# Decay levels of a gated linear attention, two at a time, with their subtractions on GpSimd

## The chip, the cores and the metric

One core of one Trainium2 chip runs the kernel. The metric is device microseconds from start to end of one execution; the time before is the median of three runs.

## The reference, cut to what matters

A two-layer encoder trunk on 256 tokens of width 1024. Each layer is a half-step SwiGLU block, a mixer, and another half-step SwiGLU block, all with RMS normalization and a residual. The mixer of layer 0 is a bidirectional gated linear attention with 4 heads (key width 128, value width 256); that of layer 1 is a differential softmax attention. The change touches only the mixer of layer 0:

```
b = cumsum(log_a)                       # per head and key column, log_a <= 0
o_i = sum over j<=i of (q_i * exp(b_i - b_j)) . k_j v_j     # forward
# backward: the same on flipped tokens, with its own gate and j<i
# then: o = rms_norm(o_f + o_b) * silu(g) @ w_out
```

## The kernel before, in words

All weights stream from HBM as float32 tiles (`stage`, three buffers) and are split into a high and a low half, so that TensorE can multiply in a faster format with three products: ScalarE writes the high half and VectorE the low half (both at line 192, `issue`, made by `parts`), into `w` tiles with five buffers. `next_weights` loads and splits ahead, up to LOOK_SPLIT = 3 weights beyond the one in use (`split_weights`, line 177). `state["hold"]` can keep back low halves until a `release`.

In `gla` the two heads of a pair (`hp` 0 or 1) and the two blocks of 128 tokens are laid side by side. The decays exp(b_i - b_j) are not formed for all pairs i, j. Tokens whose positions in a block first differ at bit s are handled as level s: both q and k are multiplied by the exponential of their distance to the middle of their group of 2s tokens, and one product of q and k gives the scores of that level. There are levels 64, 32, 16, 8, 4, 2, 1 inside a block and a level 128 across the blocks, in the order of GLA_LEVELS, "64 32 16 128 8 4 2 1", for hp 0 and then for hp 1: 16 levels. Each has three steps:

- `d` (`decay`, line 685): the differences of prefix sums go to the tile `arg` (line 710; line 706 for level 1, two smaller ones), then ScalarE writes exponentials to `qkd` (lines 712 and 713, or 707), a tile with three buffers. Level 128 needs no differences.
- `l` (`level_scores`, line 716): VectorE multiplies `qkd` by q and k (line 721; 719 for level 1), and TensorE makes eight 128-column products in one PSUM tile (`scores`, line 681).
- `t` (`take`, line 726): VectorE (line 735) or ScalarE copies the part of the scores that belongs to the level into `sd` or `sx`.

The order in which all this is issued is written out by hand in GLA_ORDER. `h` is the next half group of the projections: for v and g a half group is 12 multiplications of 512 columns (lines 231 to 233), four to a group: v0, g0, v1, g1 (v0/0 is the first of v0). `p0` and `p1` make the prefix sums (copied by ScalarE at line 669), `r0` and `r1` the raw scores, `a0` and `a1` the product with v and its sums of squares (`attend`; statistics at line 756, then a chain of small VectorE steps), `hold` sets low halves to wait, and behind the bar `x` releases them, `g0`/`g1` are gates, `o0` normalizes (line 804, then transposes at line 811). TensorE, VectorE, ScalarE and GpSimd each work through their own queue in order.

Of the kernel before, what the change touches and what calls it, by code (L numbers as in the profile page):

```python
# [11 lines left out]
F32 = mybir.dt.float32  # L12
# [3 lines left out]
ALU = mybir.AluOpType  # L16
AX = mybir.AxisListType

P = 128
# [6 lines left out]
GH, DK, DV = 4, 128, 256  # L26
# [25 lines left out]
GLA_COLS = "q0 k0 q1 k1 v0 g0 v1 g1"  # L52
GLA_LEVELS = "64 32 16 128 8 4 2 1"
GLA_ORDER = """
h z h y h h h h p0 h p1 h r0 d h d l h d l h t d l h t d l h t d r1 h t d l l h d l h t t d l h t l d h t d d h t l l a0 t d l h t d l h t hold d l h t d l t l t t | g0 h x a1 o0 h g1
"""

DIFF_COLS = "a0 a1 a2 b0 a3 v2 v3"
# [62 lines left out]
def trunk(ctx: ExitStack, tc: tile.TileContext, ins, out):  # L121
    nc = tc.nc
# [77 lines left out]
    def next_weights():  # L200
        n = state["use"]
        state["use"] += 1
        prefetch(n)
        split_weights(n)
        return split.pop(n)
# [110 lines left out]
    x = xpool.tile([P, KD, T], F32, tag="x", name="x")  # L316
# [277 lines left out]
    def gla(norm, nxt, w2):  # L594
        QK = KD // 2
        with ExitStack() as gctx:
# [5 lines left out]
            z = gp.tile([P, 4, 512], F32, tag="v", name="z")  # L602
            la = gp.tile([P, 4, 512], F32, tag="g", name="la")
            with tc.tile_pool(name="glb", bufs=2) as lp:

                lr = lp.tile([P, T], FR, tag="lr", name="lr", bufs=1)
                bias = lp.tile([P, 2, GH * DK], F32, tag="arg", name="bias", bufs=1)
                nc.sync.dma_start(bias, ins["gla_b_gate"][0].rearrange("a b -> (a b)").partition_broadcast(P))
                state["hold"] = "low"
                w = next_weights()  # L610
# [74 lines left out]
                def decay(hp, level):  # L685

                    a = lp.tile([P, 2, 4, P], F32, tag="qkd", name=f"qkd{level}_{hp}", bufs=3)
                    if level == P:
                        pf, pb = pre[:, hp, 0], pre[:, hp, 1, :, 1 : P + 2]
                        for b in range(2):  # L690
                            g0, g1 = 2 * b, 2 * b + 1
                            nc.scalar.activation(a[:, 0, g0, :], pb[:, g0, 0:P], AF.Exp, scale=-1.0, bias=pb[:, g0, P : P + 1])
                            nc.scalar.activation(a[:, 1, g0, :], pf[:, g0, 1 : P + 1], AF.Exp, scale=-1.0, bias=pf[:, g0, P : P + 1])
                            nc.scalar.activation(a[:, 0, g1, :], pf[:, g1, 1 : P + 1], AF.Exp)
                            nc.scalar.activation(a[:, 1, g1, :], pb[:, g1, 0:P], AF.Exp)
                        return a
                    s, n = level, P // (2 * level)
                    arg = lp.tile([P, 2, 4, P], F32, tag="arg", name=f"arg{level}_{hp}", bufs=1)
                    sums = pre[:, hp].rearrange("p d g c -> p (d g) c")
                    own = sums[:, :, 1 : P + 1].rearrange("p g (n w) -> p g n w", w=2 * s)  # L700
                    if s == 1:

                        aq = arg[:, 0].rearrange("p g (n w) -> p g n w", w=2)
                        for d in range(2):
                            dg = slice(4 * d, 4 * d + 4)
                            nc.vector.tensor_tensor(out=aq[:, :, :, 1 - d : 2 - d], in0=own[:, dg, :, 1:2], in1=own[:, dg, :, 0:1], op=ALU.subtract)
                        nc.scalar.activation(a[:, 0], arg[:, 0], AF.Exp)
                        return a
                    middle = sums[:, :, 0:P].rearrange("p g (n w) -> p g n w", w=2 * s)[:, :, :, s : s + 1].broadcast_to([P, 8, n, 2 * s])
                    nc.vector.tensor_tensor(out=arg.rearrange("p d g (n w) -> p (d g) n w", w=2 * s), in0=own, in1=middle, op=ALU.subtract)  # L710
                    to, by = (z.rearrange("p d g (n w) -> p d (g n) w", w=2 * s) for z in (a, arg))
                    nc.scalar.activation(to[:, :, :, s : 2 * s], by[:, :, :, s : 2 * s], AF.Exp)
                    nc.scalar.activation(to[:, ::-1, :, 0:s], by[:, :, :, 0:s], AF.Exp, scale=-1.0)
                    return a
# [48 lines left out]
                def level(what):  # L763
                    i = at[what]
                    at[what] += 1
                    if what == "d":
                        a[i] = decay(*steps[i])
                    elif what == "l":
                        ps[i] = level_scores(*steps[i], a[i])
                    else:  # L770
                        return take(*steps[i], ps.pop(i))
# [270 lines left out]
    with tc.tile_pool(name="gatew", bufs=1) as gw:  # L1042
        w2 = gw.tile([P, 2, GH * DK], FR, name="w2")
        norm = ffn(norm, 1, first=gate0, beside=lambda: load_gate(w2))
        norm = gla(norm, 2, w2)
# [47 lines left out]
```

## Time and profile before

| | us |
|---|---|
| median of three runs (lowest to highest) | 995.04 (994.36 to 996.09) |
| the profiled execution, its own time | 995.94 |
| its span in the trace | 994.10 |
| TensorE busy in the span | 983.7 |
| VectorE busy in the span | 745.6 |
| ScalarE busy in the span | 565.3 |
| GpSimd busy in the span | 1.4 |

The profiled execution lasted 1.84 us more than its span, which is what lies around it. Busy times are sums over instructions; work on different engines overlaps.

### The profile page before, as it was taken

The page shows a single profiled execution, that of the slowest core. Times are in us where ns is not written, and L with a number is a line of the kernel's source. Part 1 is how long each engine was busy: PE and PEld are TensorE (multiplying, and loading weights), DVE is VectorE, ACT ScalarE, POOL GpSimd, SP SyncE. Part 2 cuts the span into 40 slices and gives each one's busy share as a digit, 9 for nine tenths or more (in the row PEclk, how much of TensorE's full clock was granted, in tenths as well). Part 3 has the DMA queues.
Part 4 walks back from the last instruction along what each step waited for, and adds up shares of the span by engine and source line. Part 5 has one row for each costly group of instructions (what it writes and reads, how often), then busy time and mean ns, then how long its engine had stood idle before and what let it go on. Part 6 is the DMA issues. An engine that isn't in the chain of part 4 may idle for free.

```text
span 994.1 us, 14886 instructions
## 1 busy us (share of the span) xinstructions
PE 983.7 (99%) x5890; PEld 871.5 (88%) x5890; DVE 745.6 (75%) x1275; ACT 565.3 (57%) x946; POOL 1.4 (0%) x9
## 2 busy tenths in 40 slices
PE   9999999999999999999999999999999999999998
PEld 8788888998889888888888888888788998888887
DVE  6988757499977997875679787556998699877640
ACT  6756545298756765643456555435486567665430
POOL 0000000000000000000000000000000000000000
PEclk9999999999999999999999999999999999999999
DMA  9776554665322775555557555475661258755530
GB/s 307 249 241 197 170 180 123 192 220 183 123 85 85 254 253 178 193 164 185 171 176 247 194 187 174 134 230 174 228 191 66 82 183 260 236 170 177 184 127 22
DMA packets 166787, 178.87 MB, mean 180 GB/s; under 512 B 4579, under 2 KB 155550, under 8 KB 166718
## 3 DMA queue, kind: packets, MB, share of 16 engines
q1 hardware_dynamic: 166318, 177.71, 55.3%
q8 instruction: 46, 0.75, 0.3%
q10 hardware_dynamic: 400, 0.21, 0.1%
q14 instruction: 23, 0.19, 0.1%
HBM read 176.84 MB, written 1.06 MB: 179 GB/s over the span
## 4 chain that ended last, share of the span: by engine, by line
PE 69%; DVE 4%; ACT 2%; issue 1%; DMA 0%; SPq 0%; ACTq 0%
PE ps_u L216 12%; PE ps_g L216 12%; PE ps_d L216 8%; PE ps_g L217 6%; PE ps_u L217 6%; PE ps_d L217 4%; PE ps_d L232 2%; PE ps_d L231 2%; PE ps_d L233 2%; DVE w L192 2%; PE ps_s L681 1%; PE ps_w L209 1%; PE ps_w L210 1%; PE ps_w L211 1%; PE ps_g L231 1%; PE ps_g L233 1%
## 5 line engine op out<-in xcount | busy, mean ns | idle before, releaser
L192 DVE TENSOR_TENSOR w<-stage,w 128x1024 fp32r<-128x1024 f32 x332 | 384.2, 1196 | 32.9 <-ACT w L192 32.7
L192 ACT ACTIVATE w<-stage 128x1024 fp32r<-128x1024 f32 x332 | 326.9, 1036 | 61.6 <-DMA stage<-in_ffn_w_gu_dram 16.1
L216 PE MATMUL ps_g<-x,w 128*128 128x512 f32 x704 | 246.6, 392 | 0.8 <-ACT w L506 0.8
L216 PE MATMUL ps_u<-x,w 128*128 128x512 f32 x704 | 246.3, 392 | 0.0
L217 PE MATMUL ps_u<-x,w 128*128 128x256 f32 x704 | 196.9, 280 | 0.0
L217 PE MATMUL ps_g<-x,w 128*128 128x256 f32 x704 | 196.5, 280 | 0.0
L216 PE MATMUL ps_d<-a,w 128*128 128x512 f32 x528 | 183.2, 390 | 0.0
L216 PEld LDWEIGHTS ps_g<-x,w 128*128 128x128 f32 x704 | 132.0, 188 | 30.5 <-ACT w L506 1.1
L216 PEld LDWEIGHTS ps_u<-x,w 128*128 128x128 f32 x704 | 132.2, 188 | 29.0
L217 PE MATMUL ps_d<-a,w 128*128 128x256 f32 x528 | 148.9, 282 | 0.0
L217 PEld LDWEIGHTS ps_g<-x,w 128*128 128x128 f32 x704 | 132.0, 188 | 0.3
L217 PEld LDWEIGHTS ps_u<-x,w 128*128 128x128 f32 x704 | 132.2, 188 | 0.0
L216 PEld LDWEIGHTS ps_d<-a,w 128*128 128x128 f32 x528 | 99.1, 188 | 20.8
L217 PEld LDWEIGHTS ps_d<-a,w 128*128 128x128 f32 x528 | 99.8, 189 | 0.0
L327 ACT ACTIVATE x<-x,par 128x256 fp32r<-128x256 f32 x40 | 20.0, 507 | 117.3 <-DVE x L380 117.3
L256 ACT COPY half<-ps_u 128x256 f32<-128x256 f32 x88 | 32.5, 370 | 81.8 <-PE ps_u L217 80.9
L256 ACT COPY half<-ps_g 128x256 f32<-128x256 f32 x88 | 32.1, 368 | 73.1 <-PE ps_g L217 72.2
L257 DVE TENSOR_TENSOR gate<-ps_g,half 128x256 f32<-128x256 f32 x88 | 36.6, 420 | 38.6 <-ACT half L256 38.6
L257 DVE TENSOR_TENSOR up<-ps_u,half 128x256 f32<-128x256 f32 x88 | 36.6, 420 | 36.4 <-ACT half L256 36.4
L380 DVE SCALAR_TENSOR_TENSOR x<-ps_d,x 128x256 f32<-128x256 f32 x48 | 20.3, 423 | 57.9 <-PE ps_d L217 56.6
L232 PE MATMUL ps_d<-w,a 128*128 128x512 f32 (+1 forms) x110 | 38.2, 347 | 0.0
L231 PE MATMUL ps_d<-w,a 128*128 128x512 f32 (+1 forms) x110 | 38.2, 347 | 0.0
(241 smaller groups left out, 1344.2 us busy)
## 6 DMA issues: line engine op xcount, KB each, us to landing
stage<-in_ffn_w_gu_dram SPq DMA_DIRECT2D x86, 1024.0 KB, 5.2
stage<-in_ffn_w_down_dram SPq DMA_DIRECT2D x34, 1024.0 KB, 5.3
stage<-in_gla_w_in_dram SPq DMA_DIRECT2D x12, 1024.0 KB, 6.7
stage<-in_ffn_w_down_dram SPq DMA_DIRECT2D x12, 768.0 KB, 4.4
stage<-in_diff_w_in_dram SPq DMA_DIRECT2D x16, 512.0 KB, 5.0
stage<-in_gla_w_out_dram SPq DMA_DIRECT2D x4, 1024.0 KB, 5.5
stage<-in_diff_w_in_dram SPq DMA_DIRECT2D x4, 1024.0 KB
stage<-in_diff_w_out_dram SPq DMA_DIRECT2D x4, 1024.0 KB, 5.7
```

Of the source, the lines that this page charges most:

```text
L192: op()
L209: mm(ps, lhsT=w[:, k, 0, ms], rhs=act[:, k, 0, :], start=first, stop=False)
L210: mm(ps, lhsT=w[:, k, 0, ms], rhs=act[:, k, 1, :], start=False, stop=False)
L216: mm(ps, lhsT=w[:, wk, 0, ms], rhs=act[:, k, :, :], start=first, stop=False)
L217: mm(ps[:, 0:T], lhsT=w[:, wk, 1, ms], rhs=act[:, k, 0, :], start=False, stop=last)
L231: mm(ps, lhsT=act[:, k, 0, ts_], rhs=w[:, wk, 0, cs], start=k == 0, stop=False)
L232: mm(ps, lhsT=act[:, k, 0, ts_], rhs=w[:, wk, 1, cs], start=False, stop=False)
L233: mm(ps, lhsT=act[:, k, 1, ts_], rhs=w[:, wk, 0, cs], start=False, stop=k == nk - 1)
L256: nc.scalar.copy(h[:, b, :], ps[:, T:512])
L257: nc.vector.tensor_tensor(out=out_t[:, b, :], in0=ps[:, 0:T], in1=h[:, b, :], op=ALU.add)
L327: high = nc.scalar.activation(self.x2[:, d, 0, :], src, AF.Copy, scale=g)
L380: nc.vector.scalar_tensor_tensor(out=x[:, d, :], in0=ps[:, h * T : (h + 1) * T], scalar=coef, in1=x[:, d, :], op0=ALU.mult, op1=ALU.add,)
```

## The change

GLA_ORDER is rewritten: the first two `d` stand ahead of a pair of half groups, and from then on the steps come as `l d l d h h t t`, two levels between two half groups. The attend of hp 0 and the hold move later. The differences (lines 706 and 710) are issued on GpSimd where VectorE made them. The tile tag `arg`, which the gate's bias shares, gets two buffers.

```diff
 GLA_ORDER = """
-h z h y h h h h p0 h p1 h r0 d h d l h d l h t d l h t d l h t d r1 h t d l l h d l h t t d l h t l d h t d d h t l l a0 t d l h t d l h t hold d l h t d l t l t t | g0 h x a1 o0 h g1
+h z h y h h h h p0 h p1 h r0 d d h h l d l d h h t t l d l d h h t t l d l d h h t t r1 l d l d h h t t l d l d h h t t l d l d h h t t l d l d h hold t t a0 l l t t | g0 h x a1 o0 h g1
 """
...
-                bias = lp.tile([P, 2, GH * DK], F32, tag="arg", name="bias", bufs=1)
+                bias = lp.tile([P, 2, GH * DK], F32, tag="arg", name="bias", bufs=2)
...
-                    arg = lp.tile([P, 2, 4, P], F32, tag="arg", name=f"arg{level}_{hp}", bufs=1)
+                    arg = lp.tile([P, 2, 4, P], F32, tag="arg", name=f"arg{level}_{hp}", bufs=2)
...
-                            nc.vector.tensor_tensor(out=aq[:, :, :, 1 - d : 2 - d], in0=own[:, dg, :, 1:2], in1=own[:, dg, :, 0:1], op=ALU.subtract)
+                            nc.gpsimd.tensor_tensor(out=aq[:, :, :, 1 - d : 2 - d], in0=own[:, dg, :, 1:2], in1=own[:, dg, :, 0:1], op=ALU.subtract)
...
-                    nc.vector.tensor_tensor(out=arg.rearrange("p d g (n w) -> p (d g) n w", w=2 * s), in0=own, in1=middle, op=ALU.subtract)
+                    nc.gpsimd.tensor_tensor(out=arg.rearrange("p d g (n w) -> p (d g) n w", w=2 * s), in0=own, in1=middle, op=ALU.subtract)
```

## Rows read from the trace of the kernel before

**Rows 1.** The page's busy times over the span: us, share, instructions.

```profile
span 994.1 us, 14886 instructions
PE 983.7 (99%) x5890; PEld 871.5 (88%) x5890; DVE 745.6 (75%) x1275; ACT 565.3 (57%) x946; POOL 1.4 (0%) x9
```

**Rows 2.** Windows: length, busy us by engine (instructions), TensorE clock, DMA share, GB/s.

```profile
222.00:235.00 13.00, 12.77 (x88) 11.45 (x87) 12.40 (x12) 11.53 (x24) 0.00 (x0) 1.00 0.72 238
...
sum 64.00, PE 63.77 PEld 55.93 DVE 59.23 ACT 47.67 POOL 0.00; mean PE 21.26 PEld 18.64 DVE 19.74 ACT 15.89 POOL 0.00
...
300.00:700.00 400.00, 400.00 (x2349) 354.65 (x2347) 296.50 (x457) 219.84 (x340) 0.00 (x0) 1.00 0.59 190
```

**Rows 3.** TensorE's waits, 195 to 320 us: in total, times, longest.

```profile
PE ps_s L681 <- DVE qkd L721: 0.2, 1, 0.2
```

**Rows 4.** Chain of waits, 240 to 275 us: start, length, piece.

```profile
241.85 0.89 PE ps_s L681 x8
242.74 0.23 PE ps_g L231
...
245.50 0.89 PE ps_s L681 x8
...
249.15 1.78 PE ps_s L681 x16
...
269.13 0.43 PE ps_av L749 x2
...
272.59 0.89 PE ps_s L681 x8
```

**Rows 5.** Groups by line and shape, 195 to 320 us: busy, mean ns, idle before.

```profile
L192 DVE TENSOR_TENSOR w<-stage,w 128x1024 fp32r<-128x1024 f32 x32 | 37.5, 1218 | 0.9 <-ACT w L192 0.9
...
L721 DVE TENSOR_TENSOR qkd<-qkd,qk 128x1024 f32<-128x1024 f32 x14 | 16.9, 1218 | 0.0
L710 DVE TENSOR_TENSOR arg<-pre 128x1024 f32<-128x1024 f32 x12 | 14.6, 1219 | 1.3 <-ACT qkd L713 1.2
...
L712 ACT ACTIVATE qkd<-arg 128x512 f32<-128x512 f32 x12 | 7.6, 635 | 3.4 <-DVE arg L710 3.3
L713 ACT ACTIVATE qkd<-arg 128x512 f32<-128x512 f32 x12 | 7.5, 628 | 0.0
...
L706 DVE TENSOR_TENSOR arg<-pre 128x256 f32<-128x256 f32 x4 | 1.6, 424 | 0.0
```

**Rows 6.** Timeline of GpSimd, whole span: start, length, instruction.

```profile
50.86 0.95 POOL L306 MEMSET w2t<- 128x1024 f32 x1 [50.42 <-ACT a L583]
```

**Rows 7.** Timeline of TensorE, the first raw scores.

```profile
226.62 1.05 PE L681 MATMUL ps_s<-qk 128*128 128x128 f32 x8
```

**Rows 8.** Timeline of ScalarE, 220 to 236 us.

```profile
220.03 1.06 ACT L669 COPY pre<-ps_p 128x512 f32<-128x512 f32 x2
...
225.99 0.63 ACT L713 ACTIVATE qkd<-arg 128x512 f32<-128x512 f32 x1
...
231.35 0.62 ACT L712 ACTIVATE qkd<-arg 128x512 f32<-128x512 f32 x1
```

**Rows 9.** Timeline of VectorE, 220 to 236 us: low halves.

```profile
220.30 2.35 DVE L192 TENSOR_TENSOR w<-stage,w 128x1024 fp32r<-128x1024 f32 x2
...
223.71 2.35 DVE L192 TENSOR_TENSOR w<-stage,w 128x1024 fp32r<-128x1024 f32 x2
```

**Rows 10.** Timeline of VectorE, the end of the stage.

```profile
288.24 1.65 DVE L804 SCALAR_TENSOR_TENSOR o<-ps_av,ro_y,g_tm 128x256 f32<-128x256 f32 x4
292.49 0.17 DVE L756 TENSOR_SCALAR ovar<-otot 128x4 f32<-128x4 f32 x1 [2.60 <-ACT osq L754]
...
295.83 0.16 DVE L268 SCALAR_TENSOR_TENSOR ro_y<-ro_t,ro_y 128x4 f32<-128x4 f32 x1
```

More of the change, by code (lines that the diff above doesn't have):

```diff
@@ L54 @@
 GLA_ORDER = """
-h z h y h h h h p0 h p1 h r0 d h d l h d l h t d l h t d l h t d r1 h t d l l h d l h t t d l h t l d h t d d h t l l a0 t d l h t d l h t hold d l h t d l t l t t | g0 h x a1 o0 h g1
+h z h y h h h h p0 h p1 h r0 d d h h l d l d h h t t l d l d h h t t l d l d h h t t r1 l d l d h h t t l d l d h h t t l d l d h t t l d l d h hold t t a0 l l t t | g0 h x a1 o0 h g1
 """
```

## The prediction

> **What bounds the kernel now.** I read the page's busy times first: TensorE is busy 983.7 of 994.1 us [rows 1]; in the windows that I asked for, its granted clock is 1.00 [rows 2]. So a change can gain only where TensorE waits, or where it gets less to do. The reader should then go to the stage that the change touches, linear attention's levels, 222 to 286 us. There TensorE is busy 63.8 of 64 us, VectorE 59.2, ScalarE 47.7 and GpSimd nothing [rows 2]. VectorE is close to full, which invites taking work from it; but the list of TensorE's waits from 195 to 320 us has a single entry, 0.2 us for one product on VectorE (line 721) [rows 3]. VectorE's load costs 0.2 us today. That is the whole prize in this stage.
>
> The chain of waits gives the step sizes on TensorE: one level's score multiplications take 0.89 us, two in a row 1.78, a half group 2.76 (242.74 to 245.50), the first attend step 3.46 (269.13 to 272.59) [rows 4].
>
> **The change, part by part.**
>
> *Order.* TensorE's work is the same list: 24 half groups, 16 levels, two raw scores, two attends. Pairing leaves fewer turns between half groups and scores. Two levels in a row cost 1.78 and one 0.89 [rows 4], so a turn costs nothing that these rows show: 0 us.
>
> *Subtractions.* VectorE loses twelve of 1.22 us and four of 0.42 [rows 5]; 14.6 + 1.6 = 16.2 us of busy time. It was idle 4.8 us in this stage and made TensorE wait 0.2, so the gain is 0.2 us, no more.
>
> GpSimd gains them. No row has it reading two tensors. Below, its one large memset, which only writes 1024 columns, takes 0.95 us [rows 6]; three streams (two reads, a write) one after another would be 2.85. I take the two reads in series, 1.9 us, nearer to the memset because the write can go beside. Does that fit? I lay the new order out on TensorE from the first raw scores at 226.62 [rows 7] with the sizes above: half groups v0/0 and v0/1 end at 233.03, and there the scores of level 64 begin; level 32's follow at 233.92; then two half groups, two levels, and so on. Levels 8 and 4 of hp 0 start at 247.63 and 248.52, those of hp 1 at 274.96 and 275.85; the last half group of the head ends at 279.5, attend 0 at 282.96, levels 2 and 1 start at 282.96 and 283.85.
>
> GpSimd can begin when the first prefix sums are copied, 221.09 [rows 8]. Two buffers of arg let it stay two subtractions ahead: the next one needs only the exponentials of the one two before. Behind a subtraction come two exponentials (0.63 us each) and the product (1.22) [rows 5], 2.5 in all. The tightest deadline is level 4 of hp 1: by then eleven large subtractions and the two small ones of hp 0's level 1 (half of a large one, by width) must be through: 221.09 + 11.5 S + 2.5 = 275.85, S = 4.54 us. Level 32 of hp 0 gives 221.09 + 2 S + 2.5 = 233.92, S = 5.2; level 4 of hp 0, the fifth, gives S = 5.0. So a subtraction may take 4.5 us and TensorE never waits, 2.4 times my 1.9 and 1.6 times the upper bound. Cost 0, hidden by the two half groups (5.5 us) ahead of each pair; beyond 4.5 us each further microsecond costs up to 11.5 us.
>
> The Trainium skill (GPSIMD Engine Reference, 3.1) measures a two-input addition of 2048 columns at 4497 ns; my estimate from it is 2.25 us for 1024, and the sum with it is the same, since it too is under 4.5. No run here shows it yet.
>
> *New waits.* ScalarE's exponentials now wait for GpSimd. Behind them in its queue stand the copy of the raw scores, two high halves of a weight and the next level's exponentials; who waits for those is VectorE's low halves, the staging buffer and through it SP's loads. The split runs three weights ahead (LOOK_SPLIT): what is split at v0/0, at 223.7 on VectorE [rows 9], is the second half of g0's weight, used at 244.9. Those 20 us cover a late ScalarE; without them it would cost what the exponentials are late. qkd keeps three buffers, so the exponentials of level i+3 wait for the scores of level i. From there 0.9 + 5.5 + 0.9 = 7.3 us of TensorE work lie ahead of the scores of i+3, against 2.5 of exponentials and product: 4.8 us to spare.
>
> *Attend 0 later, hold later.* Attend 0 moves from before level 128 of hp 1 to after its level 4, ending at 283. Its squares and the small VectorE chain behind them (292.49 to 296.0 for the other pair, 3.5 us [rows 10]) then end near 287.7, and the first two of normalize(0)'s four products (1.65 us [rows 10]) near 288.6; their transposes come on TensorE after half group g1/2 (to 287.5) and attend 1 (to 291.0). 2.4 us to spare; with that gone, each microsecond late counts in full. The hold now follows g1/1, so that weight's two low halves (2.3 us) are made in place and not after the release; VectorE, 16 us lighter, has the room. Cost 0. The second arg buffer moves no data: 0.
>
> Sum: 0.2 us less TensorE wait. The profiled execution took 995.94 with a span of 994.10, so 1.84 lie around it, and it stands 0.90 above the median of 995.04. From the median: 995.04 - 0.23 = **994.8 us**.
>
> **What could take this away: VectorE and GpSimd getting in each other's way.** The trace of before has GpSimd idle in this stage [rows 2], so nothing in it bounds this. Lower end: none, or they share evenly. Even then the early burst fits: VectorE's four operations up to level 64's product (three low halves and the product, 4.6 us) at half speed from 221.1 end at 230.3, before 233.03. Upper end: they take turns, whole instructions at a time. GpSimd then gets the turn at 221.44, after the first low half of the 220.30 pair [rows 9]; low halves and products at 1.14 (two overlap to 2.35 [rows 9]), subtractions at 1.9: subtraction 64 to 223.34, low 224.48, 32 to 226.38, low 227.52, 16 to 229.42 (its buffer is free after the exponentials of 225.99, at 226.6 [rows 8]), low 230.56, 8 to 232.46, and only then level 64's product, 233.6. That is 0.6 us past 233.03. One more subtraction (level 4, ready when level 16's exponentials are through, which began at 231.35 before [rows 8]) goes to 235.5, and the product of 32 ends at 236.64 where TensorE wanted it at 234.49: 2.1 more, 2.7 us in all. With 2.85 for the subtraction the same steps give 237.4 (4.4 late) and 241.4 against 238.3 (3.1 more): 7.5 us. Later the two buffers hold GpSimd back, and of the later pairs only three have two large subtractions. I take none as likeliest, because it needs strict turns with GpSimd always served next; VectorE being served first would end the early products near 231.
>
> **Rivals.**
>
> 1. *Turns (slower).* As just worked out: place, the products of levels 64 and 32 of hp 0, which become TensorE's wait; price 2.7 to 7.5 us, 997.5 to 1002.5, middle 1000. It decides from about 1.6 us per subtraction on: level 64's product ends at 226.0 + 4 S, and from 232.4 (level 16's exponentials through, level 4's subtraction ready) level 32's product loses one more turn. For it: VectorE is full from the start of the stage, and three low halves stand in its queue ahead of the first product though nothing needs them for 14 us. The Trainium skill speaks for it (SBUF — State Buffer, Who interferes with whom): a VectorE instruction with two SBUF inputs and a GpSimd one that reads SBUF exclude each other, the second waiting for the whole of the first. By that rule the change would be slower; no run of before shows it. Chance 0.33.
>
> 2. *GpSimd becomes the bound (slower).* Over 4.5 us per subtraction; at 6 us, 11.5 x 1.5 = 17 us, 1012. Against it, the 0.95 us memset. Chance 0.05.
>
> 3. *The tail is late (slower).* Attend 0's statistics miss their 2.4 us; a miss of 3 more gives 998. Chance 0.03.
>
> 4. *A gain (faster).* VectorE's relief shortens something that TensorE waits for outside this stage; but from 300 to 700 us TensorE is busy 400 of 400 us [rows 2], so 992 would need shorter multiplications, and no edit shortens one. Chance 0.04.
>
> **How the numbers follow.** No change has 0.55: 994.8, own range 993.8 to 996.6. About 0.2% (2 us) is what a measurement can tell from no change. Slower: 0.33 + 0.05 + 0.03 = 0.41; faster 0.04. The range for 8 in 10 takes the first case and most of rival 1, leaving out its top, rival 2 and the gain: 993.8 to 1001.5.
>
> **What would show it.** Right: GpSimd with 16 subtractions of 1 to 3 us in the stage, VectorE's busy time there down by some 15 us, TensorE's waits for line 721 at 0 to 0.3 us, the stage as long as before, out-projection beginning at the same time. Right in size only: subtractions of 3 to 4.5 us, still no wait. Wrong by rival 1: the products (721) or low halves (192) on VectorE longer than 1.22 us beside GpSimd, and a TensorE wait for 721 at 233 to 238. By rival 2: TensorE waits that recur at each pair, with GpSimd back to back. By rival 3: a wait at the transposes of line 811.

## The result, and the profile after

The changed kernel took 1002.05 us (median of 6 runs, 1000.16 to 1004.83) against 995.5 for the kernel before (6 runs): ratio 1.0061, interval 1.005 to 1.0071. It is slower, by about 6 us, half a microsecond beyond the top of the range. Rival 1, the turns, is what happened, but not at the place that it named.

TensorE's waits from 195 to 320 us after (in total, times, longest), against 0.2 us in [rows 3]:

```profile
PE ps_s L681 <- DVE qkd L721: 4.5, 3, 1.9
```

Still products on VectorE (line 721), now 4.5 us. Windows of the stage after, as in [rows 2]: length, busy us of TensorE, its weight loads, VectorE, ScalarE, GpSimd with instruction counts, clock, DMA share, GB/s.

```profile
222.00:286.00 64.00, 59.54 (x332) 51.77 (x331) 59.60 (x44) 43.56 (x77) 34.74 (x16) 0.97 0.45 146
...
235.00:265.00 30.00, 26.40 (x137) 22.56 (x136) 30.00 (x23) 18.72 (x29) 14.63 (x8) 0.94 0.51 167
```

Look at VectorE, the third of the busy times. It gave away sixteen subtractions and is as busy as before: 59.60 us of 64, where it was 59.23, and 30.00 of 30 in the middle. GpSimd is busy 34.7 us. TensorE lost 4 us in 64.

Where VectorE's relief went stands in the groups by line and shape after, 195 to 320 us (busy, mean ns, idle before), against [rows 5]:

```profile
L192 DVE TENSOR_TENSOR w<-stage,w 128x1024 fp32r<-128x1024 f32 x32 | 48.4, 1552 | 0.9 <-ACT w L192 0.9
L710 POOL TENSOR_TENSOR arg<-pre 128x1024 f32<-128x1024 f32 x12 | 32.5, 2722 | 43.3 <-ACT pre L669 25.3 <-ACT qkd L713 15.1 <-ACT qkd L707 3.0
...
L721 DVE TENSOR_TENSOR qkd<-qkd,qk 128x1024 f32<-128x1024 f32 x14 | 22.8, 1637 | 3.3 <-ACT qkd L713 3.0 <-ACT qkd L695 0.2
```

Same counts, same shapes, longer: the low halves by 48.4 - 37.5 = 10.9 us, the products by 22.8 - 16.9 = 5.9. That is 16.8 us back on VectorE for the 16.2 taken off it. These busy times include the time for which an instruction is held up.

How one such instruction grows is seen in the timelines. GpSimd's first five subtractions one by one, and the first of hp 1; then VectorE (start, length, instruction, idle before):

```profile
219.90 4.21 POOL L710 TENSOR_TENSOR arg<-pre 128x1024 f32<-128x1024 f32 x1 [25.27 <-ACT pre L669]
224.07 1.93 POOL L710 TENSOR_TENSOR arg<-pre 128x1024 f32<-128x1024 f32 x1
225.97 2.94 POOL L710 TENSOR_TENSOR arg<-pre 128x1024 f32<-128x1024 f32 x1
228.87 3.00 POOL L710 TENSOR_TENSOR arg<-pre 128x1024 f32<-128x1024 f32 x1
231.82 2.89 POOL L710 TENSOR_TENSOR arg<-pre 128x1024 f32<-128x1024 f32 x1
...
244.61 2.24 POOL L710 TENSOR_TENSOR arg<-pre 128x1024 f32<-128x1024 f32 x1 [0.62 <-ACT qkd L713]
```

```profile
218.85 3.48 DVE L192 TENSOR_TENSOR w<-stage,w 128x1024 fp32r<-128x1024 f32 x3
225.33 1.75 DVE L721 TENSOR_TENSOR qkd<-qkd,qk 128x1024 f32<-128x1024 f32 x1 [3.00 <-ACT qkd L713]
227.22 2.77 DVE L721 TENSOR_TENSOR qkd<-qkd,qk 128x1024 f32<-128x1024 f32 x1
229.92 3.03 DVE L192 TENSOR_TENSOR w<-stage,w 128x1024 fp32r<-128x1024 f32 x1
232.87 2.92 DVE L721 TENSOR_TENSOR qkd<-qkd,qk 128x1024 f32<-128x1024 f32 x1
...
236.32 4.04 DVE L192 TENSOR_TENSOR w<-stage,w 128x1024 fp32r<-128x1024 f32 x2
240.28 1.21 DVE L721 TENSOR_TENSOR qkd<-qkd,qk 128x1024 f32<-128x1024 f32 x1
...
243.44 4.49 DVE L192 TENSOR_TENSOR w<-stage,w 128x1024 fp32r<-128x1024 f32 x2
```

GpSimd's first subtraction starts at 219.90, in the middle of three low halves that run at their usual pace to 222.33, and ends at 224.11, 1.8 us after them. The second subtraction, with VectorE idle from 222.33 to 225.33, takes 1.93 us: that is the bare price. From 225.33 on the two engines' instructions end by turns, one of each: VectorE at 227.08, 229.99, 232.95 and 235.79, GpSimd at 228.91, 231.87 and 234.71. The work that takes VectorE 1.22 us by itself lasts 2.77 to 3.03 there, and the subtractions last 2.89 to 3.00.

TensorE's timeline after shows the three waits, each for a product, and what followed the second:

```profile
241.55 1.16 PE L681 MATMUL ps_s<-qkd 128*128 128x128 f32 x8 [1.69 <-DVE qkd L721]
```

```profile
250.96 1.56 PE L681 MATMUL ps_s<-qkd 128*128 128x128 f32 x8 [1.91 <-DVE qkd L721]
252.17 0.77 PE L231 MATMUL ps_g<-w,x 128*128 128x512 f32 x1
...
253.17 0.63 PE L233 MATMUL ps_g<-w,x 128*128 128x512 f32 x1
253.60 0.63 PE L231 MATMUL ps_g<-w,x 128*128 128x512 f32 x1
...
280.87 1.13 PE L681 MATMUL ps_s<-qkd 128*128 128x128 f32 x8 [0.86 <-DVE qkd L721]
```

```profile
251.50:254.90 3.40, 3.40 (x13) 2.82 (x12) 3.40 (x3) 1.15 (x2) 2.10 (x2) 0.50 0.37 102
```

The first is for level 128 of hp 0, whose product (240.28) stood behind two low halves that took 4.04 us; the second for its level 4; the third for level 4 of hp 1. In the kernel that ran, one half group and not two stands ahead of levels 8 and 4 of hp 1: the new order line as printed under "The change" has one `h` more there, while the prediction's layout (274.96) counts one.

After the second wait the multiplications start 0.43 us apart and not 0.23. The window 251.5 to 254.9 us has the granted clock at 0.50, the lower of its two levels (1.2 GHz): 3.4 us of work at half speed, so 1.7 us on top of the waits. From the first raw scores to the first transposes (line 811), by their starts on TensorE's timeline, there are 226.62 to 291.36 before and 225.17 to 296.02 after: 64.7 and 70.9 us. I call this the stage's length from here on. It grew by 6.1 us: 4.5 us of waits against 0.2, and 1.7 for the clock, account for it. (The stage began 1.4 us earlier in that execution, which is why the spans, 994.1 and 999.0, differ by less.) The clock did not fall in every execution: two of the six had it in full throughout and took 1000.16 and 1001.91 us, so most of the loss is the waits.

### The profile page after: what moved, and what is told of

Same layout as the page of the kernel before. It is cut to its first block, busy times and chain, and to the rows that moved or that the text cites. A ratio compares the mean times of both kernels' runs of the same rounds, so it can differ in the third digit from the quotient of the medians.

```text
span 999.0 us, 14901 instructions
## 1 busy us (share of the span) xinstructions
PE 985.0 (99%) x5890; PEld 872.6 (87%) x5890; DVE 748.3 (75%) x1259; ACT 564.8 (57%) x946; POOL 38.2 (4%) x25
## 4 chain that ended last, share of the span: by engine, by line
PE 89%; DVE 6%; ACT 2%; issue 1%; DMA 1%; SPq 0%; DVEq 0%; ACTq 0%
PE ps_g L216 16%; PE ps_u L216 16%; PE ps_d L216 12%; PE ps_g L217 8%; PE ps_u L217 8%; PE ps_d L217 6%; DVE w L192 3%; PE ps_d L232 2%; PE ps_d L231 2%; PE ps_d L233 2%; PE ps_w L209 1%; PE ps_w L210 1%; PE ps_w L211 1%; PE ps_s L681 1%; ACT s L940 1%
## 5 line engine op out<-in xcount | busy, mean ns | idle before, releaser
L192 DVE TENSOR_TENSOR w<-stage,w 128x1024 fp32r<-128x1024 f32 x332 | 395.1, 1228 | 33.2 <-ACT w L192 32.9
```

The lines of the kernel that those rows point to most:

```text
L192: op()
```

## Experiments

Theory A: VectorE instructions that read two tensors from SBUF and GpSimd instructions that read SBUF take turns, whole instructions at a time, so that the subtractions cost VectorE about as much as they relieve it. The rivals: B, the new order; C, the exponentials' wait for GpSimd's results; D, the burst that the second buffer allows; and, about how the loss adds up, F to H. Each ratio is against executions of the kernel before from the same series, with 4 to 12 executions of the changed kernel.

**The two halves of the change.** First the order and the buffers without GpSimd:

```diff
-  nc.gpsimd.tensor_tensor(out=arg..., in0=own, in1=middle, op=ALU.subtract)   # and line 706
+  nc.vector.tensor_tensor(out=arg..., in0=own, in1=middle, op=ALU.subtract)
```

> The changed order and the second arg buffer, with the sixteen subtractions back on VectorE. Theory A (VectorE and GpSimd take turns, whole instructions at a time): GpSimd idle, no VectorE low half or product above 1.25 us, TensorE's waits for line 721 at most 1 us in total, 995 to 996.5 us, ratio 0.999 to 1.002. Theory B (the pairing of levels or the later attend costs the time): TensorE still waits 4 us or more, 1000 us or more, ratio 1.005 or more.

996.19 us, ratio 1.0005 (0.9996 to 1.0014); TensorE has no wait at all from 195 to 320 us, and the stage lasts 64.1 us. Windows: TensorE full, VectorE as full as ever.

```profile
235.00:265.00 30.00, 30.00 (x170) 26.13 (x169) 29.87 (x31) 21.52 (x39) 0.00 (x0) 1.00 0.43 141
```

So pairing, the late attend and the second buffer cost nothing that can be measured, and B falls. Then GpSimd without the order:

```diff
-h z h y h h h h p0 h p1 h r0 d d h h l d l d h h t t ...     # the order of the change, cut
+h z h y h h h h p0 h p1 h r0 d h d l h d l h t d l h t ...     # the order of before, cut; the rest as in the change
```

> The order of before, with the subtractions on GpSimd and two arg buffers. Theory A (turns): subtractions of 1.9 us where VectorE is idle and 2.3 to 4.2 where it is not, low halves and products up to 3 us, TensorE waits of 3 to 9 us, 998 to 1005 us, ratio 1.003 to 1.010; with one half group between levels and not two, a late product has less cover, so rather more than the change itself. Theory B (the order costs the time): ratio 0.998 to 1.002.

1000.74 us, ratio 1.0053 (1.0039 to 1.0067). One wait of TensorE for line 721 in this stage, of VectorE's first product of the stage; then the chain of waits, with the lower clock behind it (start, length, piece):

```profile
PE ps_s L681 <- DVE qkd L721: 3.1, 1, 3.1
```

```profile
228.88 2.93 DVE qkd L721
...
231.95 1.13 PE ps_s L681 x8
...
233.36 0.43 PE ps_v L232
...
236.96 0.23 PE ps_v L232
```

The stage lasts 69.2 us, 4.5 more than before. This run was expected to cost rather more than the change, whose ratio is 1.0061; it did not (the intervals overlap). The price belongs to GpSimd in either order.

**Is it the wait for results, or the turns?** GpSimd does work that nobody waits for, in the kernel before:

```diff
   nc.vector.tensor_tensor(out=arg..., in0=own, in1=middle, op=ALU.subtract)
+  spare = lp.tile([P, 2, 4, P], F32, tag="spare", bufs=1)
+  nc.gpsimd.tensor_tensor(out=spare..., in0=own, in1=middle, op=ALU.subtract)
```

> The kernel before, with the twelve large subtractions done a second time on GpSimd into a spare tile that nothing reads; VectorE's own subtractions stay. Nothing waits for GpSimd's results. Theory A (turns): VectorE's work of 59 us in a stage of 64 is held up by about 12 times 1.9 us less what falls into gaps, so TensorE waits 10 to 20 us, ratio 1.010 to 1.020. Theory C (what costs is the exponentials' wait for GpSimd's results, not the engines' turns): ratio 0.999 to 1.002.

1015.26 us, ratio 1.0201 (1.0187 to 1.0215), at the very top of what A gave; TensorE waits 14.0 us in three places and the stage lasts 83.3 us. No wait for results can be the cause here, so C falls. Groups of that run, 215 to 300 us; even VectorE's own subtractions, unchanged in the code, lengthen from 1219 ns [rows 5]:

```profile
L712 POOL TENSOR_TENSOR spare<-pre 128x1024 f32<-128x1024 f32 x12 | 37.3, 3112 | 26.0 <-ACT pre L669 25.1
L192 DVE TENSOR_TENSOR w<-stage,w 128x1024 fp32r<-128x1024 f32 x18 | 26.4, 1508 | 0.0
L710 DVE TENSOR_TENSOR arg<-pre 128x1024 f32<-128x1024 f32 x12 | 20.3, 1692 | 1.2 <-ACT qkd L715 1.2
```

**What of GpSimd's work collides?** One read instead of two, in the same place:

```diff
+  for _ in range(2):
+      nc.gpsimd.tensor_copy(spare..., sums[:, :, 1 : P + 1])
```

> The kernel before, with two copies of 128x1024 prefix sums into a spare tile on GpSimd at each of the twelve places: one read per copy where a subtraction reads two tensors. Nothing waits for them. Theory A for any read: VectorE's low halves, subtractions and products lengthen to 1.5 to 3 us while the copies run, ratio 1.008 to 1.025, as with the spare subtractions (1.020). If it takes two reads to collide: durations of 1.22 us, ratio 0.999 to 1.002.

1009.12 us, ratio 1.0128 (1.0114 to 1.0143). One read is enough: copies and VectorE's two-input instructions end by turns again, lasting about 1.9 and up to 2.06 us. And none:

```diff
+  for _ in range(2):
+      nc.gpsimd.memset(spare, 0.0)
```

> The kernel before, with two memsets of 128x1024 on GpSimd (about 1.9 us together) at each of the twelve places, into a spare tile that nothing reads. The same GpSimd time as in the run with spare subtractions, but no reads. Theory A in the form that only reads collide: VectorE's durations as before, ratio 0.999 to 1.002. If writes collide too: ratio 1.010 or more, as with the spare subtractions. Theory C: 0.999 to 1.002.

997.16 us, ratio 1.0016 (1.0008 to 1.0025), but this run tells nothing on the question: with nothing to wait for, all 24 memsets ran before the stage, and TensorE lost 1.3 us waiting for one ahead of the gate logits (line 657).

```profile
194.36 24.26 POOL L713 MEMSET spare<- 128x1024 f32 x24
```

So the memsets were tied into the chain, in the new order with all subtractions on VectorE:

```diff
+  for _ in range(2):
+      nc.gpsimd.memset(arg, 0.0)
   nc.vector.tensor_tensor(out=arg..., in0=own, in1=middle, op=ALU.subtract)
```

> The changed order and two buffers with the large subtractions on VectorE, and ahead of each of the twelve two memsets of the whole arg tile on GpSimd, which the subtraction must wait for. GpSimd stands in the chain with about 1.9 us per level, as in the change, but reads nothing. Theory A (turns, for reads): VectorE's durations stay at 1.22 us, TensorE waits at most 1 us in the stage, ratio 0.999 to 1.002. Theory C (the time goes to waiting for GpSimd's results): TensorE waits 3 us or more, ratio 1.004 or more. If writing alone collides too, low halves of 2 us or more show it.

995.96 us, ratio 0.9997 (0.9989 to 1.0006), no wait of TensorE in the stage. Windows and groups of that run:

```profile
222.00:286.00 64.00, 64.00 (x377) 56.57 (x377) 60.23 (x68) 47.31 (x86) 19.06 (x20) 1.00 0.49 163
```

```profile
L192 DVE TENSOR_TENSOR w<-stage,w 128x1024 fp32r<-128x1024 f32 x32 | 37.7, 1218 | 0.9 <-ACT w L192 0.9
...
L711 POOL MEMSET arg<- 128x1024 f32 x24 | 22.9, 956 | 51.1 <-ACT qkd L715 40.9 <-DVE z L658 8.6 <-ACT qkd L707 0.9
```

GpSimd works 19 us beside a VectorE busy 60.2 of 64, stands in every large level's chain with 1.9 us, and costs nothing. So memsets, which only write, do not collide here, and the chain has room for 1.9 us of GpSimd. That is C refuted from the other side.

**How does the loss add up?** One buffer:

```diff
-  tag="arg" ... bufs=2
+  tag="arg" ... bufs=1
```

> The change with one arg buffer, so GpSimd cannot start a subtraction before the exponentials of the one before are through. Theory A (turns): the same sixteen subtractions collide with the same VectorE work, only spread; TensorE waits 3 to 8 us, ratio 1.003 to 1.009. Theory D (it is the burst of five at the start, which the second buffer allows, that blocks VectorE): at most 1.5 us of waits, ratio 0.999 to 1.002.

1001.56 us, ratio 1.006 (1.0048 to 1.0072), waits of 3.3 us in total: D falls. Then the low halves behind the products:

```diff
-... r0 d d h h l d l d h h t t l d l d h h t t l d l d h h t t r1 ...
+... r0 d d h hold h l d l d h h t t l d l free d hold h h t t l d l free d h h t t r1 ...
+  elif step == "free": release(state["product"])     # the product issued last
```

> The change, with the low halves of three weights held until the products of the pair are issued (those of levels 16 and 128, then 8 and 4, then 2 and 1), so that VectorE's urgent work does not stand behind work that nothing needs for some 10 us. GpSimd's subtractions and VectorE's list are the same. Theory A with the queue as its cause (a product waits behind low halves that are themselves held up by a subtraction): TensorE waits at most 2 us, ratio 1.000 to 1.003. Theory F (the two engines together have more to do than the stage has time for, so order doesn't matter): waits of 3 us or more, perhaps for a low half and not for a product, ratio 1.004 to 1.008.

1001.55 us, ratio 1.006 (1.0047 to 1.0074), outside what A gave and within F's range. The wait for level 128 is gone, but the held low halves came due together, four of them in 9.85 us, and the products behind them were late instead. TensorE's waits for line 721 and VectorE's timeline:

```profile
PE ps_s L681 <- DVE qkd L721: 3.6, 3, 2.1
```

```profile
236.85 1.21 DVE L721 TENSOR_TENSOR qkd<-qkd,qk 128x1024 f32<-128x1024 f32 x1
...
245.22 9.85 DVE L192 TENSOR_TENSOR w<-stage,w 128x1024 fp32r<-128x1024 f32 x4
...
255.61 1.22 DVE L721 TENSOR_TENSOR qkd<-qkd,qk 128x1024 f32<-128x1024 f32 x1
```

So this order moves the wait and leaves the sum, as F has it. But the edit holds low halves only twice, up to the products of levels 128 and 4 of hp 0. The third hold that the expectation names, up to levels 2 and 1, is not in it, and the longest wait (2.1 us, up to 256.97) came at level 2, behind the four low halves that the second `free` let go. An order that holds them throughout was not tried. Then half of the change at a time:

```diff
-  nc.gpsimd.tensor_tensor(...)
+  (nc.gpsimd if hp else nc.vector).tensor_tensor(...)     # second pair only; first pair only: swapped
```

> The change, with the subtractions of hp 0 back on VectorE and those of hp 1 on GpSimd: half the collisions, and none in the burst at the start. Theory A: VectorE operations above 1.5 us only after 245 us, TensorE waits 0 to 3 us, ratio 1.000 to 1.003. Theory B (the late attend or the pairing): ratio 1.005 or more.

996.72 us, ratio 1.0006 (0.9998 to 1.0014); one wait, 1.0 us.

> The change, with the subtractions of hp 0 on GpSimd and those of hp 1 back on VectorE; with the run of the second pair only it splits the price. The second pair alone made no measurable difference (1.0006). Theory A: the collisions fall where low halves, products and five subtractions come together at the start, so this half carries the price: TensorE waits of 3 to 5 us before 252 us, ratio 1.003 to 1.006. If the price needs both halves (a shortfall that builds up over the stage): ratio 1.000 to 1.002.

996.93 us, ratio 1.0013 (1.0004 to 1.0022); waits of 1.9 us in total. A's number for this run is missed, and the alternative in it came: 0.06% and 0.13% for the halves, 0.61% for the whole. The stages of the profiled executions show where the rest lies. Against the 64.1 us of the run with all subtractions on VectorE they last 65.3 (second pair), 66.5 (first pair) and 70.9 (both): 1.2, 2.4 and 6.8 more. Of the 3.2 that the halves leave open, about 1.7 is the lower clock, which neither half has in this stage, and the rest is waits (4.5 against 1.0 + 1.9). Where do these waits come from? In this run the two low halves after 243 us take 2.77, in the change 4.49, since hp 1's first subtraction (244.61) runs ahead into them. Hence the last run:

```diff
+  (nc.vector if hp and level in (64, 32) else nc.gpsimd).tensor_tensor(out=arg..., ...)
```

> The change, with only the subtractions of levels 64 and 32 of hp 1 back on VectorE; the other fourteen stay on GpSimd. Alone, the first pair's subtractions cost 0.13% and the second's 0.06%, both together 0.61%. Theory G (the two add up because hp 1's first subtractions run ahead, thanks to the second buffer, into VectorE's backlog of hp 0): without these two the wait near 249 us shrinks to under 0.5 us, TensorE waits 1.5 to 3 us in all, ratio 1.001 to 1.0035. Theory H (it is the number of subtractions, wherever they fall; fourteen of sixteen left): ratio 1.0045 to 1.006.

1000.59 us, ratio 1.0046 (1.0032 to 1.006). G's place was right, its price wrong: the wait near 249 us shrank from 1.9 to 0.2 us (VectorE had those two low halves in 2.77 again), yet TensorE waits 4.0 us in all. The 1.7 for level 128 of hp 0 and the 0.8 near 281 us stayed as they were, and a new one of 1.3 us came at 268 us:

```profile
PE ps_s L681 <- DVE qkd L721: 4.0, 4, 1.7
```

The ratio lies outside G's range and at the lower end of H's; its interval overlaps that of the change. The stage lasts 69.0 us, 1.8 less than in the change, and that is about what the lower clock cost there, which this execution does not have in the stage. So taking two subtractions back moved a wait and hardly shortened the waits together. That VectorE can catch up in the other pair's half of the stage when one pair alone is on GpSimd, and cannot with both, is my reading of these runs; none measured it.

## Why the prediction was wrong

What held: TensorE had 0.2 us to win and nothing else, so no gain was to be expected, and none came (the new order with VectorE's subtractions lands at 1.0005). A subtraction takes 1.93 us by itself, against 1.9 taken (the second estimate, 2.25, was above it); that two reads in series are the reason was not tested. GpSimd in the chain is covered by the half groups: the memset run puts 1.9 us there at no cost. Attend 0, the hold and the second buffer cost nothing.

What failed is the step that priced the subtractions at nothing: "So a subtraction may take 4.5 us and TensorE never waits". The 12 large ones averaged 2.72 us, well under 4.5, and TensorE waited 4.5 us. The bound let GpSimd take its time but put the product at its bare 1.22 us right behind the exponentials. The product stands in VectorE's queue, behind low halves that a subtraction holds up (4.04 us for two, ahead of level 128), and is held up itself. VectorE, which was to be "16 us lighter", was as busy as before.

The turns were thought of, and then set aside: "I take none as likeliest, because it needs strict turns with GpSimd always served next". At the first meeting VectorE was indeed served, three low halves in a row, and GpSimd waited 2.4 us; the products of levels 64 and 32 ended at 227.08 and 229.99, before their scores at 231.71, and were not late as the rival had it. But from 225.33 on the turns were strict, one instruction of each, and the later meetings, passed over with "Later the two buffers hold GpSimd back", are where the time went. The even sharing that served as lower end was tested on the first 9 us alone. A sum over the stage was to be had from the same rows and sizes: 59.2 - 16.2 + 13 x 1.9 (the four small subtractions counted as one large) = 67.7 us of turns in a stage of 64. As an estimate of the loss, if none of it falls into gaps, that is 3.7 us; the waits came to 4.5.

The price of rival 1, 2.7 to 7.5 us, holds the 6 us measured, but that is luck: it was worked out for two products that were not late. The waits came for levels 128 and 4 of hp 0 and level 4 of hp 1, and 1.7 us of the loss is the lower clock after a wait, which the prediction had not counted. Its chance of 0.33 was too low, and the range ended half a microsecond short. The rule cited for it, the Trainium skill's (SBUF — State Buffer, Who interferes with whom), agrees with these runs: two-input VectorE work and reading GpSimd work held each other up (1.22 to 3.0 us), memsets did not (1.218).

What stays open: the two pairs cost 0.19% apart and 0.61% together, and of that the profiled executions show the lower clock (1.7 us) and 1.6 us more of waits; why these waits grow is not shown, since no run measured VectorE's backlog itself. That the engines take turns is read from durations and timelines; no run tells how a turn is granted. Whether low halves held back throughout would save the products is untried.

## What to carry to other kernels

Before an engine is relieved, look at what waits for it: VectorE was 92% full here and cost TensorE 0.2 us. Work moved from VectorE to GpSimd was no relief here, because GpSimd read SBUF while VectorE took two tensors from it. In such a case count the moved instruction's whole time against VectorE, over the whole stage, and not only at the first deadline. A deadline for GpSimd alone is not enough: the product behind it has VectorE's queue to pass. Memsets, which only write, cost VectorE nothing in the one run that had them beside it.

## What the runs showed of the hardware

- A 128x1024 float32 subtraction on GpSimd takes 1.93 us beside an idle VectorE and up to 4.21 us beside a busy one; its duration in the profile includes the time it is held up.
- One read is enough for the collision: copies on GpSimd cost 1.28%. Memsets did not collide: VectorE's low halves stayed at 1.218 us.
- VectorE's copies of scores out of PSUM (line 735), which take only the mask from SBUF beside them, were not held up: 0.744 us before, 0.737 after. One starts at 254.74, inside a subtraction (253.90 to 256.63), and lasts 0.74; the level 1 product right behind it, with two tensors from SBUF, lasts 1.81 where it took 0.68.
- GpSimd's first instruction of the stage waited while VectorE's instructions came one right after another: 4.21 us in the change, 6.62 with the spare subtractions, 5.88 with the copies. After VectorE's first pause none of GpSimd's subtractions or copies in these three runs lasted over 3.00 us.
- A wait of 1.91 us on TensorE was followed by half the clock (granted 0.50) for six multiplications (0.43 us apart), one of 3.1 us in the old order likewise. One of 1.69 us in the change and one of 1.70 in the run of the first pair were not, yet in the old order one of 1.19 us, at 720 us, was: in these rows the length of the wait alone does not decide it.
